# Products of a tile of zeros on TensorE, at the head and around the second normalization of one transformer block

## The chip, the cores and the metric

One core of a Trainium2 chip runs the kernel. A core has five engines, each with a queue of its own that it works off in order: TensorE (PE, matrix products, with its weight loads as PEld), VectorE (DVE), ScalarE (ACT), GpSimd (POOL) and SyncE (SP, which here issues the transfers of the weights). Each waits for the others by semaphores. The metric is the time of one execution on the device in microseconds; lower is better. TensorE's clock has two levels, 1.2 and 2.4 GHz; the profile shows the granted clock as a share of the higher one.

## The reference

One layer of a diffusion transformer in float32: 256 latent tokens and 256 context tokens of 2048 features, 16 heads of 128, and a gated feed-forward part of 5504 features. Cut to what the change touches:

```python
sh1, sc1, g1, sh2, sc2, g2 = adaln(c, w_ada, b_ada)        # silu(c) @ w_ada + b_ada, in six parts
h  = modulate(rms_norm(x, g_mix), sh1, sc1)                # x * (1 + scale) + shift
hc = modulate(rms_norm(ctx, g_mix), csh1, csc1)            # the same of the context
y, _ = neighbourhood_attention(h, hc, w_qkv, ...)          # q, k, v from h; k, v from hc too
x  = x + g1 * y
hf = modulate(rms_norm(x, g_ffn), sh2, sc2)                # the second normalization
x  = x + g2 * conv_ffn(hf, w_up, conv_w, conv_b, w_down)
```

rms_norm divides each token by the root of the mean of its squares over all 2048 features.

## The kernel before, in words

Activations lie with features on the partitions, as 16 blocks of 128 features by 256 tokens. A product of float32 operands is made from high and low parts: `wpair` (L147) loads a weight tile of two blocks of rows by 512 columns over SP, ACT casts it to its high part `wh` (L155), DVE subtracts to get the low part `wl` (L156; two slots). A product is then three: high by high, low by high, high by low. Activations are split the same way: ACT writes the high part (`hh`, L450; `hf`, L817), DVE the low part (L451, L818).

The order in each engine's queue is not the order of the text. A scheduler simulates the program on a time line of its own (L954) and appends each instruction where its simulated time comes, so a change in one place can move instructions of other engines. What the queues hold is fixed when the program is built.

**The head.** `start` code at L485 to L505 streams the latent tokens `xl` in chunks, squares them on ACT (`stats`, L360), adds them on DVE (L365), sums over the partitions on TensorE (`col_sums`, L227) and makes the reciprocal root rstd in `rstd_rows`: scale on DVE (L208), a power on POOL (L195), a Newton step on DVE (L196 to L200), a diagonal matrix (L213, tiles `xd` or `cd`), a product with ones that spreads it over all partitions (L218), a copy (L220, `xb` or `cb`). The context `xc` goes the same way. In parallel `ada_step` (L395) makes shift and scale of one or two blocks: four loads `wx` of `w_ada` (L405, four slots, each of two transfers), four groups of four small products (L411), a copy `ev` on ACT (L418), transposes on TensorE (L421), reductions on DVE (L426 to L434). `modulate` then makes a block of normalized activations (L445 DVE, L450 ACT, L451 DVE), and `first_products` (L459) multiplies it with k and v weights (`nat`: L378, L379, L380). The first block goes alone, the second alone, then pairs. PSUM has eight banks: four under the tag `pj`, two `ms`, two `mx`.

**The second normalization.** Behind the output projection each block gets gate and residual (L778), is squared on ACT (L783) and scaled into `xg` (L788). `col_sums` (L789) takes the last two squares and the sum of the others; `rstd_rows` (L795) makes `yb` the way above, with tile `yd`. A loop over the 16 blocks makes `t` (DVE L815, or POOL L813 for most odd ones), the high part on ACT (L817) and the low part on DVE (L818) of `hf`. The up projection (`proj`, L713, called at L888) follows: each step takes two blocks and eight pairs of products, `wh` with both parts (L728, 512 columns) and `wl` with the high part (L732, 256 columns). The weight splits of L155 and L156 stand in the same queues of ACT and DVE as the loop.

## Time and profile before

| | us |
|---|---|
| Runs | 1459.02, 1455.05, 1456.06 (median 1456.06) |
| Span of the profiled execution, first to last instruction | 1455.1 |
| TensorE busy / weight loads | 1405.5 (97%) / 1166.9 (80%) |
| DVE / ACT / POOL busy | 1004.8 (69%) / 782.6 (54%) / 285.2 (20%) |
| Mean granted clock of TensorE | 0.991 |

Busy time is the time in which an engine works on an instruction; it overlaps between engines. The profile comes from one execution. In the timeline rows the first number is the start, the second the time from the first start to the last end of a group of equal instructions, then engine, line, operation, output and inputs, shapes, and the count; in brackets stands how long the engine was idle ahead of it and what released it. A product is listed with a time longer than its distance to the next, since products are pipelined: the distance of starts is what it costs in a row.

### The profile page before, as it was taken

To read this page: it belongs to the slowest core of one execution; us is meant where nothing else is said; L and a number is where in the kernel's file an instruction comes from. 1 tells how busy PE (TensorE), PEld (TensorE's weight loads), DVE (VectorE), ACT (ScalarE), POOL (GpSimd) and SP (SyncE) were. 2 spreads that over 40 slices of the span, in tenths; PEclk is the share of its full clock that TensorE was granted. 3 is DMA by queue.
4 is the path that set the end of the run, shared out by engine and by line. 5 is a ranking of instruction groups with operands and counts; after the bars stand their busy time and mean duration, and the time that the engine had idled before them with its cause. 6 is when DMAs were issued, how large, how long until landed. Compare 5 with 4: busy or idle time off the path is not lost.

```text
span 1455.1 us, 21097 instructions
## 1 busy us (share of the span) xinstructions
PE 1405.5 (97%) x7608; PEld 1166.9 (80%) x7608; DVE 1004.8 (69%) x1541; ACT 782.6 (54%) x1356; POOL 285.2 (20%) x208
## 2 busy tenths in 40 slices
PE   5999999999998999999899999999999999999998
PEld 2665787778787887788788888888888888888888
DVE  4556587687868778766868878788777775545454
ACT  4322265676565676664656656666665654333333
POOL 1000025465445556200201111111111000000000
PEclk9999999999999999999899999999999999999999
DMA  9999547687667777445567776777776556566554
GB/s 308 357 329 319 176 141 250 199 260 220 213 222 246 223 247 244 151 152 175 183 193 230 224 238 222 244 219 228 233 230 193 183 175 206 185 202 205 167 170 156
DMA packets 208920, 317.14 MB, mean 218 GB/s; under 512 B 23360, under 2 KB 87744, under 8 KB 208816
## 3 DMA queue, kind: packets, MB, share of 16 engines
q1 hardware_dynamic: 208688, 315.79, 68.1%
q8 instruction: 59, 0.97, 0.3%
q14 instruction: 45, 0.37, 0.1%
q10 hardware_dynamic: 128, 0.01, 0.0%
HBM read 312.75 MB, written 3.01 MB: 217 GB/s over the span
## 4 chain that ended last, share of the span: by engine, by line
PE 66%; DVE 12%; issue 10%; DMA 7%; ACT 2%; POOL 2%; SPq 1%; DVEq 0%; POOLq 0%; ACTq 0%
PE pj L728 15%; PE pj L732 8%; PE mx L728 7%; PE ms L728 6%; DVE wl L156 4%; PE pj L379 4%; PE pj L378 4%; PE pj L380 4%; DMA wa<-in_w_ada 4%; PE mx L732 4%; PE ms L732 3%; PE ms L411 2%; PE mx L378 2%; PE mx L379 2%; PE mx L380 2%
## 5 line engine op out<-in xcount | busy, mean ns | idle before, releaser
L156 DVE TENSOR_TENSOR wl<-wr,wh 128x1024 fp32r<-128x1024 f32 (+2 forms) x425 | 496.1, 1168 | 257.0 <-PE pj L732 86.8
L155 ACT CAST wh<-wr 128x1024 fp32r<-128x1024 f32 (+2 forms) x425 | 411.8, 970 | 406.0 <-PE pj L728 150.5
L277 POOL TENSOR_TENSOR acc<-acc,wa 128x512 f32<-128x512 f32 x144 | 226.6, 1573 | 440.9 <-issue 218.1
L728 PE MATMUL pj<-hf,wh 128*128 128x512 f32 x688 | 226.7, 397 | 2.0 <-DVE hf L818 2.0
L379 PE MATMUL pj<-wl,hh 128*128 128x512 f32 x512 | 204.8, 400 | 4.6 <-DVE wl L156 4.5
L380 PE MATMUL pj<-wh,hl 128*128 128x512 f32 x512 | 202.0, 397 | 0.0
L378 PE MATMUL pj<-wh,hh 128*128 128x512 f32 x512 | 194.4, 400 | 2.5 <-ACT hh L450 2.5
L732 PE MATMUL pj<-hf,wl 128*128 128x256 f32 x688 | 154.7, 284 | 2.2 <-DVE wl L156 1.7
L732 PEld LDWEIGHTS pj<-hf,wl 128*128 128x128 f32 x688 | 130.6, 190 | 20.6 <-DVE wl L156 6.2
L728 PEld LDWEIGHTS pj<-hf,wh 128*128 128x128 f32 x688 | 125.3, 190 | 17.7 <-DVE hf L818 2.8
L276 ACT ACTIVATE wa<-wa,sT 128x512 f32<-128x512 f32 x144 | 97.4, 718 | 77.7 <-DMA wa<-in_w_ada 68.1
L728 PE MATMUL mx<-hf,wh 128*128 128x512 f32 x352 | 124.1, 393 | 0.0
L379 PEld LDWEIGHTS pj<-wl,hh 128*128 128x128 f32 x512 | 97.8, 191 | 28.7 <-DVE wl L156 7.9
L728 PE MATMUL ms<-hf,wh 128*128 128x512 f32 x336 | 120.1, 396 | 0.0
L378 PEld LDWEIGHTS pj<-wh,hh 128*128 128x128 f32 x512 | 96.8, 190 | 27.0 <-ACT hh L450 3.4
L380 PEld LDWEIGHTS pj<-wh,hl 128*128 128x128 f32 x512 | 97.6, 191 | 19.5
L732 PE MATMUL mx<-hf,wl 128*128 128x256 f32 x352 | 84.8, 282 | 1.5 <-DVE wl L156 1.5
L279 DVE SCALAR_TENSOR_TENSOR acc<-wa,sT,acc 128x512 f32<-128x512 f32 x80 | 74.4, 931 | 10.7 <-DMA wa<-in_w_ada 10.1
L732 PE MATMUL ms<-hf,wl 128*128 128x256 f32 x336 | 81.7, 282 | 0.0
L732 PEld LDWEIGHTS mx<-hf,wl 128*128 128x128 f32 x352 | 66.3, 188 | 10.4 <-DVE wl L156 3.2
L732 PEld LDWEIGHTS ms<-hf,wl 128*128 128x128 f32 x336 | 63.3, 188 | 7.8
L728 PEld LDWEIGHTS ms<-hf,wh 128*128 128x128 f32 x336 | 63.2, 188 | 6.9
(251 smaller groups left out, 2384.7 us busy)
## 6 DMA issues: line engine op xcount, KB each, us to landing
wr<-in_w_up SPq DMA_DIRECT2D x160, 512.0 KB, 4.4
wa<-in_w_ada SPq DMA_DIRECT2D x128, 512.0 KB, 4.7
wr<-in_w_qkv SPq DMA_DIRECT2D x93, 512.0 KB, 4.9
wr<-in_w_down SPq DMA_DIRECT2D x63, 512.0 KB, 4.6
wx<-in_w_ada SPq DMA_DIRECT2D x56, 512.0 KB, 8.7
wr<-in_w_o SPq DMA_DIRECT2D x24, 512.0 KB, 3.8
wr<-in_w_down SPq DMA_DIRECT2D x45, 256.0 KB, 3.0
wr<-in_w_up SPq DMA_DIRECT2D x16, 384.0 KB, 3.4
```

The lines of the kernel that those rows point to most:

```text
L155: a = nc.scalar.copy(hi[:, :kn, :cn], w[:, :kn, :cn])
L156: b = nc.vector.tensor_tensor(out=lo[:, :kn, :cn], in0=w[:, :kn, :cn], in1=hi[:, :kn, :cn].bitcast(F32), op=ALU.subtract,)
L276: nc.scalar.mul(w[:, k, :], w[:, k, :], s)
L277: nc.gpsimd.tensor_add(acc, acc, w[:, k, :])
L279: nc.vector.scalar_tensor_tensor(out=acc, in0=w[:, k, :], scalar=s, in1=acc, op0=ALU.mult, op1=ALU.add)
L378: nc.tensor.matmul(pt, hh[:, kt, ts], wh[:, k, :], start=a, stop=False)
L379: nc.tensor.matmul(pt, hh[:, kt, ts], wl[:, k, :], start=False, stop=False)
L380: nc.tensor.matmul(pt, hl(kt, ts), wh[:, k, :], start=False, stop=z)
L411: nc.tensor.matmul(ap_[32 * k : 32 * k + 32, :n], s32[:, 4 * q + k, :], w[:, k * n : (k + 1) * n], start=(q == 0), stop=(q == 3), tile_pos ...
L728: nc.tensor.matmul(pts[b][:, : t1 - t0], wh[:, k, bs], mov(kt, slice(t0, t1)), start=(kt == 0 and t0 == 0), stop=False,)
L732: nc.tensor.matmul(pts[b][:, :T], wl[:, k, bs], mov(kt, slice(0, T)), start=False, stop=(kt == kn - 1),)
```

## The change

A tile `warm` of 128x512 zeros is filled on POOL. A helper `spin` issues n products of it (128 columns of it as the stationary operand, all 512 moving) into a PSUM bank whose content nobody reads. With `behind` it is scheduled behind a given instruction; to have these, `col_sums` and `rstd_rows` note their last product in a list `marks`. It is called in six places: 36 products ahead of the first load; 4 behind each of the first three groups of the first adaLN step and 6 behind its transposes; 8 behind the column sums of the second normalization, and 6 behind the product that spreads its rstd. The removed comments move the line numbers (L227 is now L228, L360 L375, L411 L426, L418 L435, L421 L438, L450 L469, L476 L495, L728 L748, L732 L752, L815 L837, L818 L840).

```diff
-    last, hold = [], []
+    last, hold, marks = [], [], []
...
+        ins = nc.tensor.matmul(bp, ones, dg.rearrange("p b t -> p (b t)"), start=True, stop=True)
+        marks.append(ins.ins)
...
+        marks.append(ins.ins)
         return sums
...
+    warm = cp.tile([P, CH], F32R, name="warm")
+    nc.gpsimd.memset(warm.bitcast(F32), 0.0)
+
+    def spin(n, bank, behind=None):
+
+        with ExitStack() as order:
+            if behind is not None:
+                order.enter_context(tc.issue_after(behind))
+            pt = bank()
+            for _ in range(n):
+                ins = nc.tensor.matmul(pt, warm[:, :P], warm, start=True, stop=True)
+        return ins.ins
...
+            if b0 == 0 and q < 3:
+                spin(4, ms, ins.ins)
...
+            ins = nc.tensor.transpose(sp[:, b * P : (b + 1) * P], ev[:, b * P : (b + 1) * P], ident)
+        if b0 == 0:
+            spin(6, ms, ins.ins)
...
+    spin(36, ms)
     stream(xl, xT)
...
     sums2 = col_sums(ms()[:, 0:2], tail)
+    spin(8, pj, marks[-1])
...
     rb2, rb2p, diag = rstd_rows(fp, sums2, "y", nc.scalar.copy)
+    spin(6, pj, marks[-1])
```

Because the scheduler places everything anew, other instructions move too, at the head (up to about 165 us) and behind the second normalization; elsewhere the queues hold the same in the same order.

At the head, this is ACT's queue from the first casts on before. `sq` are squares (of the context chunks `xc`), `hh` the high part of a modulated block, `ev` the adaLN sums out of PSUM, `vsum` a v product out of PSUM.

```order
L155 CAST wh<-wr 128x512 x2
L418 COPY ev<-ms 128x256
L360 ACTIVATE sq<-xc 128x512 x3
L450 ACTIVATE hh<-xl,shT 128x256
L360 ACTIVATE sq<-xc 128x512 x5
L155 CAST wh<-wr 128x512
L476 COPY vsum<-mx 128x512 x2
L418 COPY ev<-ms 128x256
L450 ACTIVATE hh<-xc,shT 128x256
```

And this the same stretch after.

```order
L155 CAST wh<-wr 128x512 x2
L435 COPY ev<-ms 128x256
L375 ACTIVATE sq<-xc 128x512 x8
L469 ACTIVATE hh<-xl,shT 128x256
L155 CAST wh<-wr 128x512
L495 COPY vsum<-mx 128x512 x2
L435 COPY ev<-ms 128x256
L469 ACTIVATE hh<-xl,shT 128x256
```

All eight squares of the context now stand ahead of the first `hh` of the latent tokens, where three stood before.

TensorE's queue from its start to the first product of weights (`wh`, `hh`), after; before, it held the same without the rows of L264.

```order
L264 MATMUL ms<-warm 128x512 x36
L426 MATMUL ms<-wx,s_120 32x256 x4
L228 MATMUL mx<-ones,sacc 128x1 x4
L426 MATMUL ms<-wx,s_120 32x256 x5
L264 MATMUL ms<-warm 128x512 x4
L426 MATMUL ms<-wx,s_120 32x256 x7
L264 MATMUL ms<-warm 128x512 x4
L218 MATMUL mx<-xd,ones 128x256
L264 MATMUL ms<-warm 128x512 x4
L438 MATMUL ms<-ident,ev 128x128 x2
L264 MATMUL ms<-warm 128x512 x6
```

The four products of zeros that belong to the first group stand in the second, and those of the third group behind the spreading product.

TensorE's queue from the end of the first twelve products to the first product of the context's block (`cd` is the diagonal of the context's rstd, `sacc` the squares), before:

```order
L380 MATMUL pj<-wh,hl_110 128x512 x2
L380 MATMUL mx<-wh,hl_110 128x512 x2
L411 MATMUL ms<-wx,s_118 32x256 x4
L227 MATMUL mx<-ones,sacc 128x1 x4
L411 MATMUL ms<-wx,s_118 32x256 x8
L218 MATMUL mx<-cd,ones 128x256
L411 MATMUL ms<-wx,s_118 32x256 x4
L421 MATMUL ms<-ident,ev 128x128 x2
```

And after, to the first product of the next blocks:

```order
L395 MATMUL pj<-wh,hl_112 128x512 x2
L395 MATMUL mx<-wh,hl_112 128x512 x2
L426 MATMUL ms<-wx,s_120 32x256 x12
L228 MATMUL mx<-ones,sacc 128x1 x4
L426 MATMUL ms<-wx,s_120 32x256 x4
L438 MATMUL ms<-ident,ev 128x128 x2
L218 MATMUL mx<-cd,ones 128x256
L426 MATMUL ms<-wx,s_120 32x512 x4
```

The column sums (L227, now L228) moved behind three groups of the next adaLN step, the spreading product (L218) behind the fourth and the transposes, and the first group of the step after that (32x512) ahead of the products.

At the second normalization, TensorE's queue from the last column sums to the first products of the up projection, before:

```order
L227 MATMUL ms<-ones,sacc_5379 128x1 x2
L227 MATMUL ms<-ones,sq 128x1 x4
L218 MATMUL mx<-yd,ones 128x256
L728 MATMUL pj<-hf,wh 128x512
L732 MATMUL pj<-hf,wl 128x256
L728 MATMUL pj<-hf,wh 128x512
```

And after:

```order
L228 MATMUL ms<-ones,sacc_5440 128x1 x2
L228 MATMUL ms<-ones,sq 128x1 x4
L264 MATMUL pj<-warm 128x512 x8
L218 MATMUL mx<-yd,ones 128x256
L264 MATMUL pj<-warm 128x512 x6
L748 MATMUL pj<-hf,wh 128x512
L752 MATMUL pj<-hf,wl 128x256
L748 MATMUL pj<-hf,wh 128x512
```

Eight products of zeros stand between the sums and the spreading product, six behind it.

DVE's queue in the loop over the blocks, from behind the fifth low part on, before:

```order
L818 SCALAR_TENSOR_TENSOR hf<-t,sh2T,hf 128x256
L815 TENSOR_TENSOR t<-xg,yb 128x256
L818 SCALAR_TENSOR_TENSOR hf<-t,sh2T,hf 128x256 x3
L815 TENSOR_TENSOR t<-xg,yb 128x256
L818 SCALAR_TENSOR_TENSOR hf<-t,sh2T,hf 128x256
L156 TENSOR_TENSOR wl<-wr,wh 128x1024
L818 SCALAR_TENSOR_TENSOR hf<-t,sh2T,hf 128x256
L815 TENSOR_TENSOR t<-xg,yb 128x256
L818 SCALAR_TENSOR_TENSOR hf<-t,sh2T,hf 128x256
L815 TENSOR_TENSOR t<-xg,yb 128x256
L818 SCALAR_TENSOR_TENSOR hf<-t,sh2T,hf 128x256
L156 TENSOR_TENSOR wl<-wr,wh 128x1024
```

And after, from the same place:

```order
L840 SCALAR_TENSOR_TENSOR hf<-t,sh2T,hf 128x256
L156 TENSOR_TENSOR wl<-wr,wh 128x1024
L837 TENSOR_TENSOR t<-xg,yb 128x256
L840 SCALAR_TENSOR_TENSOR hf<-t,sh2T,hf 128x256 x3
L837 TENSOR_TENSOR t<-xg,yb 128x256
L156 TENSOR_TENSOR wl<-wr,wh 128x1024
L840 SCALAR_TENSOR_TENSOR hf<-t,sh2T,hf 128x256 x2
L837 TENSOR_TENSOR t<-xg,yb 128x256
L840 SCALAR_TENSOR_TENSOR hf<-t,sh2T,hf 128x256
L156 TENSOR_TENSOR wl<-wr,wh 128x1024
L837 TENSOR_TENSOR t<-xg,yb 128x256
```

The first split of a weight (`wl`) stands behind the tenth `hf` before, and behind the sixth after; the following ones come earlier too.

## Rows read from the trace of the kernel before

**Rows 1.** Busy time, share of the span and number of instructions of TensorE and its weight loads and the other engines, from the page's first part.

```profile
PE 1405.5 (97%) x7608; PEld 1166.9 (80%) x7608; DVE 1004.8 (69%) x1541; ACT 782.6 (54%) x1356; POOL 285.2 (20%) x208
```

**Rows 2.** Windows by stage: stretch and its length, then busy time and instructions of PE, PEld, DVE, ACT and POOL, the granted clock of TensorE as a share of 2.4 GHz, the share of DMA and its GB/s.

```profile
23.00:28.00 5.00, 4.93 (x12) 3.79 (x12) 4.11 (x7) 3.31 (x7) 0.00 (x0) 1.00 1.12 328
28.00:36.00 8.00, 6.30 (x47) 2.46 (x45) 1.98 (x7) 1.85 (x4) 0.70 (x1) 0.79 1.13 322
36.00:53.00 17.00, 17.00 (x88) 10.19 (x87) 8.21 (x22) 7.98 (x14) 0.00 (x0) 1.00 1.08 356
704.00:707.00 3.00, 2.57 (x22) 2.28 (x20) 1.94 (x3) 1.42 (x4) 0.00 (x0) 1.00 0.92 332
707.00:713.00 6.00, 1.60 (x7) 0.83 (x6) 3.79 (x11) 3.48 (x7) 0.73 (x2) 0.54 0.90 305
713.00:717.70 4.70, 4.70 (x15) 4.02 (x16) 4.67 (x9) 2.93 (x7) 2.59 (x3) 0.50 0.50 172
717.70:730.00 12.30, 11.85 (x68) 9.96 (x68) 11.28 (x17) 7.53 (x12) 4.03 (x4) 1.00 0.34 108
```

**Rows 3.** Timeline of PE at the head.

```profile
12.27 1.08 PE L411 MATMUL ms<-wx,s 128*32 128x256 f32 x8 [12.27 <-DMA wx<-in_w_ada]
...
17.66 1.08 PE L411 MATMUL ms<-wx,s 128*32 128x256 f32 x8 [0.65 <-DMA wx<-in_w_ada]
18.66 1.22 PE L218 MATMUL mx<-xd,ones 128*128 128x256 f32 x2
19.95 0.66 PE L421 MATMUL ms<-ident,ev 128*128 128x128 f32 x2
23.07 0.79 PE L378 MATMUL pj<-wh,hh 128*128 128x512 f32 x1 [2.46 <-ACT hh L450]
...
24.09 0.63 PE L378 MATMUL pj<-wh,hh 128*128 128x512 f32 x1
24.51 0.63 PE L379 MATMUL pj<-wl,hh 128*128 128x512 f32 x1
...
28.95 1.05 PE L227 MATMUL mx<-ones,sacc 128*128 128x1 f32 x8
...
31.85 1.08 PE L411 MATMUL ms<-wx,s 128*32 128x256 f32 x8 [1.17 <-DMA wx<-in_w_ada]
32.86 1.22 PE L218 MATMUL mx<-cd,ones 128*128 128x256 f32 x2
...
36.56 0.40 PE L378 MATMUL pj<-wh,hh 128*128 128x512 f32 x1
36.80 0.40 PE L379 MATMUL pj<-wl,hh 128*128 128x512 f32 x1
...
39.95 0.50 PE L378 MATMUL pj<-wh,hh 128*128 128x512 f32 x1
```

**Rows 4.** Waits of PE from 36 to 165 us: what it waited for, us in total, times, the longest.

```profile
PE ms L411 <- DMA wx<-in_w_ada: 0.2, 1, 0.2
```

**Rows 5.** Timeline of PE around the second normalization.

```profile
706.07 1.29 PE L227 MATMUL ms<-ones,sq 128*128 128x1 f32 x8
709.72 1.19 PE L218 MATMUL mx<-yd,ones 128*128 128x256 f32 x2 [2.36 <-issue]
712.95 0.79 PE L728 MATMUL pj<-hf,wh 128*128 128x512 f32 x1 [2.04 <-DVE hf L818]
...
713.75 0.63 PE L728 MATMUL pj<-hf,wh 128*128 128x512 f32 x1
...
714.39 0.63 PE L728 MATMUL pj<-hf,wh 128*128 128x512 f32 x1
...
717.59 0.44 PE L728 MATMUL pj<-hf,wh 128*128 128x512 f32 x1
...
717.99 0.40 PE L728 MATMUL pj<-hf,wh 128*128 128x512 f32 x1
...
718.34 0.40 PE L728 MATMUL pj<-hf,wh 128*128 128x512 f32 x1
...
725.12 0.38 PE L732 MATMUL pj<-hf,wl 128*128 128x256 f32 x1 [0.45 <-DVE wl L156]
```

**Rows 6.** Timeline of POOL at the start: the fill of the mask tile and the last operation of the constants.

```profile
1.05 0.15 POOL L99 MEMSET maskt<- 128x64 f32 x1
...
2.07 0.51 POOL L108 TENSOR_SCALAR_AFFINE_SELECT maskt<-maskt 64x48 f32<-64x48 f32 x2
```

**Rows 7.** Timeline of ACT at the head.

```profile
25.00 1.15 ACT L360 ACTIVATE sq<-xc 128x512 f32<-128x512 f32 x2 [0.35 <-DMA xc<-in_ctxT]
...
35.43 0.51 ACT L450 ACTIVATE hh<-xc,shT 128x256 fp32r<-128x256 f32 x1
```

**Rows 8.** Timeline of DVE at the head, on the way of the context's rstd.

```profile
31.60 0.43 DVE L213 TENSOR_TENSOR cd<-ident,cr 128x256 f32<-128x256 f32 x1
34.12 0.42 DVE L220 COPY cb<-mx 128x256 f32<-128x256 f32 x1 [2.09 <-PE mx L218]
```

**Rows 9.** Timeline of DVE in the loop behind the second normalization: a low part, a `t` and a split of a weight.

```profile
721.39 0.47 DVE L818 SCALAR_TENSOR_TENSOR hf<-t,sh2T,hf 128x256 fp32r<-128x256 f32 x1
721.79 0.41 DVE L815 TENSOR_TENSOR t<-xg,yb 128x256 f32<-128x256 f32 x1
...
723.85 1.22 DVE L156 TENSOR_TENSOR wl<-wr,wh 128x1024 fp32r<-128x1024 f32 x1
```

More of the change, by code (lines that the diff above doesn't have):

```diff
@@ L217, in rstd_rows @@
         bp = mx()[:, :T]
-        nc.tensor.matmul(bp, ones, dg.rearrange("p b t -> p (b t)"), start=True, stop=True)
+        ins = nc.tensor.matmul(bp, ones, dg.rearrange("p b t -> p (b t)"), start=True, stop=True)
+        marks.append(ins.ins)
         rb = pool.tile([P, T], F32, tag=name + "b", name=name + "b")
@@ L226, in col_sums @@
             for b in range(2):
-                nc.tensor.matmul(
+                ins = nc.tensor.matmul(
                     sums[:, b : b + 1], sq[:, b * P : (b + 1) * P], ones[:, 0:1],
@@ L410, in ada_step @@
             for k in range(4):
-                nc.tensor.matmul(
+                ins = nc.tensor.matmul(
                     ap_[32 * k : 32 * k + 32, :n], s32[:, 4 * q + k, :], w[:, k * n : (k + 1) * n],
@@ L420, in ada_step @@
         for b in range(2 * nb):
-            nc.tensor.transpose(sp[:, b * P : (b + 1) * P], ev[:, b * P : (b + 1) * P], ident)
+            ins = nc.tensor.transpose(sp[:, b * P : (b + 1) * P], ev[:, b * P : (b + 1) * P], ident)
+        if b0 == 0:
+            spin(6, ms, ins.ins)
         blk = slice(b0, b0 + nb)
```

## Prediction

> **What bounds the kernel now.** I read the engine shares first: TensorE is busy 97% of the span [rows 1], so nearly every microsecond is products, and a change can win only where TensorE stands still or runs slowly. Next the table by stage with its granted clock [rows 2]: between 36 and 53 us TensorE is busy all of the time at full clock; the two places where it is neither are the head (up to 36 us) and the second normalization (707 to 717.7 us), where the clock column shows 0.54 and 0.50, that is mostly the lower of its two levels, 1.2 instead of 2.4 GHz.
>
> The clock can also be read from the products themselves. At the head, starts are 0.43 us apart at 24 us (24.09, 24.51) and 0.24 at 36.56 and 36.80 [rows 3], although the clock column says 1.00 between 23 and 28 us [rows 2]. By the column the head has nothing to win before 28 us; by the pitch its first twelve products, 5.3 us from 23.07 on, ran at 1.2 GHz and could win 2.5. I go by the pitch. The Trainium skill, page "TensorE: Matmul & The Clock Gate", section "Part 1: The HAM clock gate (the "warmup" mystery)", says that the throttled level is the default and that activity releases it; by that rule the head could come out 2.5 us faster, by the column 0. The pitch agrees with the rule, the column does not.
>
> Then who waits for whom. Head: TensorE starts at 12.27 when the first adaLN weights land, waits for the fourth tile until 17.66, and for the first modulated block until 23.07 [rows 3]. After 36 us it waits 0.2 us in all of the next 129 us [rows 4]: a delay that the head leaves is handed on one to one. Second normalization: the column sums end at 707.36, the product that spreads rstd over the partitions starts at 709.72, the up projection at 712.95; its pairs of products come every 0.64 us (713.75, 714.39) at first and every 0.35 us (717.99, 718.34) later [rows 5].
>
> **The change at the head.** *36 products of zeros first.* Their tile is filled on POOL, behind the last mask operation, which ends at 2.6 us; a 128x64 fill took 0.15 us [rows 6], eight times that is 1.2 at most, so they begin between 2.6 and 3.8. A product of this shape costs 0.43 or 0.24 us, 36 of them 8.6 to 15.5. At the second normalization the clock rose behind 4.64 us of products (712.95 to 717.59 [rows 5]); with as many slow ones here, 11 go at 0.43 and 25 at 0.24: 10.7 us, end at 13.3 to 14.5, one or two us behind 12.27. That is hidden: the fourth adaLN group waits for its weights until 17.66 whatever the others do. Cost 0.
>
> *The products between.* Four and four come in the gaps ahead of the spreading product (18.66), four ahead of the transposes (19.95), six behind them: 14 x 0.24 = 3.4 us, of which at most 0.6 delays the transposes and none the first product, because that waits for other engines until 23.07. Cost 0 by themselves.
>
> *What the scheduler made of it costs more.* In the new order ACT squares all eight chunks of the context before it makes the first modulated block; before, three came first. The chunks arrive as they arrive: the last two are squared from 25.00 on, 1.15 us for both, and a modulated block took 0.51 [rows 7]. So the first product moves from 23.07 to 25.00 + 1.15 + 0.51 = 26.7, **3.6 us late**, and TensorE, done with its zeros by about 22.6, has stood idle for four microseconds; I take the clock to be low again (at the second normalization it went down as TensorE stopped [rows 2, 5]). The twelve products end at 29.5 at full clock or 31.9 at low. That delay alone would be partly absorbed: before, TensorE then waited 1.17 us for weights at 31.85. But behind it the order of the context's normalization is also worse. Its column sums, at 28.95 before [rows 3], now stand behind three adaLN groups, the third of which needs the tile that landed at 31.85 (perhaps a little earlier, since the queue now asks for one more of these tiles ahead of the first split weight): start 32.4 to 33.6. And its spreading product, at 32.86 before, ahead of the fourth group, now stands behind that group and its transposes, which wait for a copy on ACT. From the sums' start, the chain to the first product took 36.0 - 28.95 = 7.0 us (sums to 30.00, the scaled diagonal to 32.03, spread to 34.12, copy, modulate and ACT to 35.94 [rows 3, 7, 8]), with about 1 us of wait in it. 6 to 7 us from 32.4 to 33.6 gives 38.4 to 40.6 for the first product of the context. From there the products take 2.8 us. Before, that work was done at 39.95, one adaLN group included that the new order has already run in the wait. Lag: 38.4 + 2.8 - 39.95 = 1.3 to 40.6 + 2.8 - 39.95 = 3.5, and up to 1 us more if these products run at 1.2 GHz for some time. Value **+3.0 us**, range +1.3 to +4.2; above the middle, since each of the three late things (squares, sums, spread) stands in one row. Nothing gives it back: TensorE is fully busy until 165 us.
>
> **The change at the second normalization.** *Eight products of zeros behind the sums.* TensorE stands idle for 2.36 us here, 707.36 to 709.72 [rows 5]. Eight at full clock are 1.9 us: hidden, done before the product that spreads rstd. At low clock they take 3.4 us and delay it by 1.1. The column's 0.54 over 707 to 713 [rows 2] is about 0.5 us at full clock and 5.5 at half: it fell near 707.5, after the sums had ended, and was full before [rows 2]; the zeros leave no idle time behind the sums, so I take the full clock.
>
> *Six behind the spreading product*: 1.4 us (2.6 at low clock) in a gap of 2.04 us (710.91 to 712.95 [rows 5]). Hidden at full clock.
>
> *What it buys.* If TensorE stays at full clock, the seven cold pairs (712.95 to 717.59, 4.64 us) take 7 x 0.35 = 2.45: 2.2 us saved. The spreading product took 1.19 us at low clock; at half that, 0.6 comes off ahead of everything. Together up to 2.8, and 0.3 more if the wait of 0.45 us at 725.12 for a low part goes too: bound -3.1.
>
> *What is late next.* DVE, which makes the low parts of activations and weights, is busy 4.67 of 4.70 us while the products are slow, and 11.28 of 12.30 after [rows 2]. A TensorE 2.8 us ahead would meet it: the low part that TensorE awaited at 725.12 was made from 723.85 on [rows 9]. In the old order the gain would stop there. But the order of DVE has changed with the simulated faster products: the first of these splits stands behind the 6th high-low pair instead of the 10th, some 3 us earlier, and its slots come free with the products. Laid out with durations from rows (0.47 a low part, 0.41 a t, 1.22 a split [rows 9], steps of eight pairs at 2.8 us), DVE keeps up with a new wait of 0.2 to 0.5 us. Value **-2.3 us**, range -3.1 to -1.0 (only half of the pairs come out fast), at worst +1.6 (below).
>
> Elsewhere, from 165 us on, each engine's order is the same. The sum is +3.0 - 2.3 = **+0.7 us**: span 1455.1 + 0.7 = 1455.8. The median of the runs shown (1456.06) lies 0.96 above the profiled span, so 1456.8 for the median. A difference under 0.3% (4.4 us) can't be told from none in a measurement of this kernel.
>
> **The rivals.**
>
> 1. *The head costs nothing and the second normalization gives all.* For it: DMA engines are fully busy until 53 us and beyond [rows 2], so arrivals may set the pace and the lag may be absorbed by earlier weights. Against: after 36 us TensorE waits 0.2 us for a weight [rows 4], so there is no wait to shorten. Time 1456.1 - 3.1 = 1453.0 to 1453.8 with the middle value: 16%. A head that is faster by the 2.5 us of its slow first products as well: 1450.6, 4%.
>
> 2. *Slower: the eight zeros run at 1.2 GHz.* The mechanism sits at 707.4 us: eight at 0.43 take 3.4 us in a gap of 2.36, the spreading product starts 1.1 late, six more at 0.43 take 2.6 in a gap of 2.04, and the first product of the up projection starts 1.6 late and no warmer. It decides from a pitch of 2.36 / 8 = 0.29 us on. For it: the clock was low from 707.5 on, 0.1 us after the sums, so it may have been on its way down with them. With the head at +3.0: 1456.06 + 4.6 = 1460.7. 12%.
>
> 3. *Zeros don't raise the clock at all.* Then 36 x 0.43 = 15.5 us push the first adaLN group from 12.27 to about 18.5, the head comes out about 12 us late, the second normalization 1.6: 1470. No row shows a product of zeros. 3%.
>
> **How the numbers follow.** Forecast 65%: 1456.8. The rivals have 16, 4, 12 and 3. Its own range: head +1.3 to +4.2, second normalization -3.1 to -1.0, mostly 1454.5 to 1459. Reaching to rival 1's middle and rival 2's edge leaves out about 15%: 1453.0 to 1460.5. Faster by over 0.3% (under 1451.7): 5%. Slower by over 0.3% (over 1460.4): 10%, rival 3 and the larger half of rival 2. The same: 85%.
>
> **What would show it.** Head right: 36 products end near 13 to 14 us; the first product of weights at about 26.7, behind ACT; the context's sums later than 32; TensorE's queue at the work of 39.95 about 3 us later. Head wrong: first product at 23 or earlier, or the lag gone by 100 us. Second normalization right: eight starts 0.24 apart, the up projection's first pairs 0.35 apart, granted clock near 1.00 from 707 to 718, DVE's first split some 3 us earlier. Wrong: pairs still 0.64 apart, or waits of over 1 us for low parts before 730 us. The prediction falls as a whole if TensorE is idle after 36 us for more than the lag, or if the head's first product isn't late.

## The result

The changed kernel took **1459.82 us** (median of 20 runs), the kernel before 1455.48 us (20 runs, measured beside it): ratio **1.003, 95% interval 1.002 to 1.0039**. It is slower, by about 4.3 us. The profiled execution has a span of 1459.1 us; before, 1455.1 us.

First the engine shares, to hold against [rows 1]:

```profile
PE 1418.4 (97%) x7676; PEld 1176.5 (81%) x7676; DVE 1002.2 (69%) x1541; ACT 782.6 (54%) x1356; POOL 281.2 (19%) x209
```

68 more products (36 + 12 + 6 + 8 + 6 of zeros), 13 us more of busy TensorE, and the share is still 97%. What counts is where they lie. Windows by stage (columns as in [rows 2], the second normalization shifted by the lag):

```profile
23.00:28.00 5.00, 1.75 (x8) 1.10 (x7) 4.75 (x10) 3.54 (x7) 0.00 (x0) 1.00 1.12 330
...
36.00:53.00 17.00, 15.66 (x70) 8.20 (x70) 6.00 (x17) 6.22 (x12) 0.00 (x0) 0.81 1.09 353
...
718.00:735.00 17.00, 16.58 (x90) 13.73 (x88) 16.36 (x27) 11.75 (x22) 7.38 (x7) 0.99 0.55 176
```

Between 23 and 28 us TensorE is now busy 1.75 us instead of 4.93, and between 36 and 53 us no longer all of the time and no longer at full clock (0.81 instead of 1.00). At the second normalization the loop runs at 0.99 from 718 us on. So the head lost and the second normalization gained; the timelines say how much. TensorE at the head, against [rows 3]:

```profile
2.64 11.08 PE L264 MATMUL ms<-warm 128*128 128x512 f32 x36 [2.64 <-POOL warm L255]
13.65 0.64 PE L426 MATMUL ms<-wx,s 128*32 128x256 f32 x8
...
26.74 0.50 PE L393 MATMUL pj<-wh,hh 128*128 128x512 f32 x1 [3.25 <-ACT hh L469]
27.08 0.40 PE L394 MATMUL pj<-wl,hh 128*128 128x512 f32 x1
27.32 0.39 PE L393 MATMUL pj<-wh,hh 128*128 128x512 f32 x1
...
32.62 0.64 PE L426 MATMUL ms<-wx,s 128*32 128x256 f32 x8 [1.17 <-DMA wx<-in_w_ada]
33.19 1.05 PE L228 MATMUL mx<-ones,sacc 128*128 128x1 f32 x8
...
38.77 1.94 PE L426 MATMUL ms<-wx,s 128*32 128x512 f32 x8 [0.54 <-DMA wx<-in_w_ada]
40.64 0.79 PE L393 MATMUL pj<-wh,hh 128*128 128x512 f32 x1
41.23 0.63 PE L394 MATMUL pj<-wl,hh 128*128 128x512 f32 x1
41.66 0.63 PE L393 MATMUL pj<-wh,hh 128*128 128x512 f32 x1
...
44.36 1.06 PE L426 MATMUL ms<-wx,s 128*32 128x512 f32 x8
```

Read it downwards. The 36 products of zeros are done at 13.65 and the adaLN groups go on behind them. The first product of weights waits 3.25 us for ACT and starts at 26.74 instead of 23.07. Its clock is high: the next two starts, 27.08 and 27.32, are 0.24 apart, where before they were 0.43. In spite of that the context's column sums start at 33.19 instead of 28.95 and its first product at 40.64 instead of 36; that product and the next go at 0.43 again (41.23, 41.66). The work that was done at 39.95 before is done at 44.36: **4.4 us late**. At 168 us the lag between the two profiled executions is 6.2 us; of the 1.8 us between, one new wait for a low part accounts for 0.4, the rest is not assigned. How far such a number can be trusted: e1, e6, e7 and e8 below have no zeros at the head and the queue of before there on TensorE, and their profiled executions lag by -0.05, 0.96, 1.66 and 0.07 us at 168 us.

What held the first product up, in the timelines of ACT ([rows 7] before) and DVE:

```profile
25.14 1.15 ACT L375 ACTIVATE sq<-xc 128x512 f32<-128x512 f32 x2 [0.30 <-DVE sacc L380]
26.20 0.49 ACT L469 ACTIVATE hh<-xl,shT 128x256 fp32r<-128x256 f32 x1
...
25.05 0.48 DVE L464 SCALAR_TENSOR_TENSOR xl<-xl,gsT,xb 128x256 f32<-128x256 f32 x1
```

The modulated block stands directly behind the last square. DVE was nearly as late: its part of the block, at 21.32 before, now stands behind four adds of the context's squares and ends at 25.5. So the late squares on ACT are not the only thing that moved ahead of this block; without them it would have come some 0.7 us earlier here.

Now the second normalization on TensorE, against [rows 5]:

```profile
712.79 1.29 PE L228 MATMUL ms<-ones,sq 128*128 128x1 f32 x8
713.94 3.05 PE L264 MATMUL pj<-warm 128*128 128x512 f32 x8
716.79 1.05 PE L218 MATMUL mx<-yd,ones 128*128 128x256 f32 x2
717.28 2.17 PE L264 MATMUL pj<-warm 128*128 128x512 f32 x6
719.88 0.50 PE L748 MATMUL pj<-hf,wh 128*128 128x512 f32 x1 [0.42 <-DVE hf L840]
...
720.33 0.40 PE L748 MATMUL pj<-hf,wh 128*128 128x512 f32 x1
...
720.69 0.40 PE L748 MATMUL pj<-hf,wh 128*128 128x512 f32 x1
...
735.34 0.38 PE L752 MATMUL pj<-hf,wl 128*128 128x256 f32 x1 [0.20 <-DVE wl L156]
```

From the sums to the spreading product are 4.00 us (3.65 before), to the first pair 7.09 (6.88 before), then the pairs come every 0.36 us at once (720.33, 720.69), where seven of them took 4.64 us before. The lag of 6.7 us at the sums is 4.6 at 731 us: **2.1 us gained**. Ahead of the sums TensorE waited 1.28 us for DVE (0.33 before; 1.51 in e2, which has no zeros here), so the lag had just risen from 5.8; counted from there the gain is 1.2. At the end of the program the lag is 4.0 us (1459.1 - 1455.1), near the 4.3 of the medians.

### The profile page after: what moved, and what is told of

Its sections match the earlier page's. It is cut to its first block, busy times and chain, and to the rows that moved or that the text cites. A ratio compares the mean times of both kernels' runs of the same rounds, so it can differ in the third digit from the quotient of the medians.

```text
span 1459.1 us, 21228 instructions
## 1 busy us (share of the span) xinstructions
PE 1418.4 (97%) x7676; PEld 1176.5 (81%) x7676; DVE 1002.2 (69%) x1541; ACT 782.6 (54%) x1356; POOL 281.2 (19%) x209
## 4 chain that ended last, share of the span: by engine, by line
PE 65%; DVE 13%; DMA 10%; issue 3%; ACT 3%; POOL 3%; SPq 1%; DVEq 0%; POOLq 0%; ACTq 0%
PE pj L748 16%; PE pj L752 9%; PE mx L748 8%; PE ms L748 7%; DMA wa<-in_w_ada 6%; DVE wl L156 5%; PE mx L752 4%; PE ms L752 4%; PE pj L394 3%; PE pj L393 2%; PE pj L395 2%; POOL acc L292 2%; PE ms L426 2%; PE mx L393 2%; PE mx L394 2%
## 5 line engine op out<-in xcount | busy, mean ns | idle before, releaser
L292 POOL TENSOR_TENSOR acc<-acc,wa 128x512 f32<-128x512 f32 x144 | 221.7, 1540 | 436.2 <-issue 218.8
L748 PE MATMUL pj<-hf,wh 128*128 128x512 f32 x688 | 224.8, 395 | 0.4 <-DVE hf L840 0.4
L752 PE MATMUL pj<-hf,wl 128*128 128x256 f32 x688 | 153.8, 283 | 2.0 <-DVE wl L156 1.4
L752 PEld LDWEIGHTS pj<-hf,wl 128*128 128x128 f32 x688 | 129.5, 188 | 20.2 <-DVE wl L156 5.9
L748 PEld LDWEIGHTS pj<-hf,wh 128*128 128x128 f32 x688 | 124.3, 188 | 15.6 <-DVE hf L840 0.9
L748 PE MATMUL mx<-hf,wh 128*128 128x512 f32 x352 | 124.2, 393 | 0.0
L748 PE MATMUL ms<-hf,wh 128*128 128x512 f32 x336 | 120.1, 396 | 0.0
L752 PE MATMUL mx<-hf,wl 128*128 128x256 f32 x352 | 84.8, 282 | 1.5 <-DVE wl L156 1.5
L752 PE MATMUL ms<-hf,wl 128*128 128x256 f32 x336 | 81.8, 282 | 0.0
L752 PEld LDWEIGHTS mx<-hf,wl 128*128 128x128 f32 x352 | 66.3, 188 | 10.4 <-DVE wl L156 3.2
L752 PEld LDWEIGHTS ms<-hf,wl 128*128 128x128 f32 x336 | 63.3, 188 | 7.9
L748 PEld LDWEIGHTS ms<-hf,wh 128*128 128x128 f32 x336 | 63.2, 188 | 6.9
```

The costliest lines, as they stand in the source:

```text
L292: nc.gpsimd.tensor_add(acc, acc, w[:, k, :])
L748: nc.tensor.matmul(pts[b][:, : t1 - t0], wh[:, k, bs], mov(kt, slice(t0, t1)), start=(kt == 0 and t0 == 0), stop=False,)
L752: nc.tensor.matmul(pts[b][:, :T], wl[:, k, bs], mov(kt, slice(0, T)), start=False, stop=(kt == kn - 1),)
```

## The experiments

The theory at the start: the loss is in the head, and it comes from the order that the scheduler chose when it counted the zeros (squares first, the context's sums and spreading product behind adaLN groups), not from the products of zeros. The rivals: the zeros themselves delay something, or the second normalization brought nothing. Diffs are against the changed kernel; line numbers differ a little from kernel to kernel. "Lag" is by how much a profiled execution is behind the profiled execution of the kernel before at the same work.

### e1: only the second normalization

```diff
-            if b0 == 0 and q < 3:
-                spin(4, ms, ins.ins)
-        if b0 == 0:
-            spin(6, ms, ins.ins)
-    spin(36, ms)
```

> Only the eight and six products of zeros at the second normalization; the head is that of before. In the changed kernel the lag fell from 6.7 us at the column sums to 4.6 us at 731 us, 2.1 us. If that gain belongs to the zeros (theory): lag 0 up to 705 us, about -2 us at 730 and at the end, 1453.5 against 1455.5, the first pairs of the up projection 0.35 apart. If it was only made possible by a head that came late, so that DVE and the transfers were further ahead (rival): within 0.5 us of before, with new waits for low parts of 1.5 us or more between 718 and 730 us.

Measured: ratio 0.9977 [0.9962, 0.9993], 1452.63 us. In its profile no lag at 168 us (-0.04), and between the sums and 731 us a gain of 1.9 us. TensorE there:

```profile
708.84 3.44 PE L264 MATMUL pj<-warm 128*128 128x512 f32 x8
...
712.57 1.76 PE L264 MATMUL pj<-warm 128*128 128x512 f32 x6
```

The eight take 3.44 us, 0.43 each: they run at the low clock. The six take 0.29 each, and the pairs come at full clock (0.35 apart). The second part of the change alone is a gain.

### e2: only the head

```diff
-    spin(8, pj, marks[-1])
-    spin(6, pj, marks[-1])
```

> Only the zeros of the head. Theory and rival both expect the whole loss of the head here: first product of weights at 26.7 us, a lag of about 6 us at 165 us. The end tells how the two places add: 1455.5 + 4.5 + 2 = 1462 if what the second normalization gives back is its own, about 1460 if the lag shrinks there by itself.

Measured: ratio 1.0033 [1.002, 1.0046], 1459.7 us; lag 5.6 us at 168 us, and from the sums of the second normalization to 731 us nearly unchanged (5.65 to 5.09), with pairs 0.64 us apart as before. The loss is the head's. In this execution the first twelve products ran at the low clock (from 27.78 on, 0.43 apart, after 3.58 us without work), and the context's first product started at 40.65 all the same, as in the changed kernel (40.64).

### e3: the new order without any zeros

```diff
+    with tc.issue_after(squares[-1]):
+        modulate(*GRAINS[0], ((0, xl),))
...
+            if b0 == 1 and q == 2:
+                with tc.issue_after(ins.ins):
+                    rb.append(sum_up(csq, "c")[0])
...
+            with tc.issue_after(marks[-2]) if b0 == 1 and q == 3 else ExitStack():
...
-    spin(36, ms)
-    spin(8, pj, marks[-1])
-    spin(6, pj, marks[-1])
```

(and the products between are left out.)

> No product of zeros anywhere, but the order of the changed kernel at the head, forced by hand: all eight squares of the context ahead of the first modulated block, the context's column sums behind three adaLN groups of the next step, its spreading product behind the fourth and the transposes. Theory (the order makes the loss): first product of weights at 26 to 27 us, lag of 5 to 8 us at 165 us (more than in the changed kernel by what low clock costs), 1460 to 1464. Rival (the zeros themselves make it, by standing in TensorE's queue and putting the first adaLN group 1.4 us later): first product late, but the lag gone by 165 us, 1455 to 1457.

Measured: ratio 1.0018 [1.0008, 1.0028], 1459.59 us, lag 4.2 us at 168 us. The head is late without one product of zeros: first product at 27.02, sums at 33.64, first product of the context at 39.93. The lag is less than was expected of the order (5 to 8 us).

### e4: all zeros, the squares and the last group put back

```diff
-            nc.scalar.activation(sq, xin[:, kt : kt + 2, :], AF.Square)
+            with tc.issue_after(gate[0]) if gate and kt >= 6 else ExitStack():
+                nc.scalar.activation(sq, xin[:, kt : kt + 2, :], AF.Square)
...
+            with tc.issue_after(marks[-1]) if b0 == 1 and q == 3 else ExitStack():
```

> All products of zeros as in the changed kernel, but the order of before at the head as far as it matters: three squares of the context, then the first modulated block, then the rest; the context's column sums behind one adaLN group, its spreading product behind three. Theory: first product of weights at 23 to 24 us at full clock, no lag or up to 2.5 us of lead at 165 us, and the 2 us of the second normalization on top: 1451 to 1453.5. Rival: the lag of 5 to 6 us at 165 us stays, 1459 to 1460.

Measured: ratio 0.9999 [0.9991, 1.0008]. Better than the change, short of e1; the time lies between what the theory and the rival expected. TensorE:

```profile
16.67 1.82 PE L264 MATMUL ms<-warm 128*128 128x512 f32 x4
...
21.35 0.59 PE L218 MATMUL mx<-xd,ones 128*128 128x256 f32 x2
...
25.47 0.50 PE L394 MATMUL pj<-wh,hh 128*128 128x512 f32 x1 [0.89 <-ACT hh L471]
...
41.53 1.06 PE L428 MATMUL ms<-wx,s 128*32 128x512 f32 x8 [1.69 <-DMA wx<-in_w_ada]
```

Here the zeros between take time in the queue: four of them at the low clock take 1.8 us, and the spreading product starts at 21.35 (18.66 before). The first product starts at 25.47 (23.07), but not by that alone: on DVE two adds of the context's squares, 0.68 us each, stand ahead of its part of the block (24.39; 21.32 before). The adaLN group behind the context's products is on time all the same (38.78; 38.96 before): the warm products have made up the 2.4 us. Then a wait of 1.69 us for weights, ahead of 41.53, makes the kernel late again.

### e5: few zeros, in the old order

```diff
-            if b0 == 0 and q < 3:
-                spin(4, ms, ins.ins)
         if b0 == 0:
-            spin(6, ms, ins.ins)
+            spin(4, ms, ins.ins)
-    spin(36, ms)
+    spin(24, ms)
```

> Zeros at the head that leave the order of before in every queue as it was, but for one spreading product and one diagonal that move by one place: 24 first and four behind the transposes, together with the eight and six at the second normalization. Theory (order made the head's loss; the zeros cost nothing, and the arrival of weights at 28 and 32 us eats what warm products win): first product of weights near 23 us at full clock, TensorE then waits for a tile of adaLN weights near 28 and 32 us, lag at 165 us between -0.7 and +0.3, end as with the zeros of the second normalization alone, 1453 to 1454. Rival (zeros cost something by themselves): lag of +1.5 to +3 at 165 us, 1455 to 1457. Second rival (the warm products' 2.5 us are kept): lag -2.5 at 165 us, 1451.

Measured: ratio 0.9979 [0.9965, 0.9993], the same as e1. TensorE:

```profile
13.62 1.08 PE L426 MATMUL ms<-wx,s 128*32 128x256 f32 x8 [3.56 <-DMA wx<-in_w_ada]
...
24.80 0.50 PE L393 MATMUL pj<-wh,hh 128*128 128x512 f32 x1 [2.21 <-ACT hh L467]
25.13 0.39 PE L394 MATMUL pj<-wl,hh 128*128 128x512 f32 x1
...
30.01 1.03 PE L426 MATMUL ms<-wx,s 128*32 128x256 f32 x8 [2.19 <-DMA wx<-in_w_ada]
```

The first adaLN tile happened to land at 13.62 instead of 12.27, so all is a good microsecond late. The first products run at full clock (24.80 to 25.13 and on at 0.23), and what that wins is waited away: 2.19 us for weights ahead of 30.01. Not all of this wait speaks of warm products, since that group is 1.6 us late (28.38 before) with the late first tile. The lag at 168 us is 2.1 us, as the rival that zeros cost something had it; the time is the theory's.

### e6: the earlier split of a weight undone

e1 with the first split in the loop behind the tenth low part, as before:

```diff
+        if kt == 9:
+            late_low.append(low.ins)
...
+                if len(seen) > 1:
+                    order.enter_context(tc.issue_after(late_low[0]))
```

> Zeros at the second normalization alone, with DVE's first split of a weight put back behind the tenth low part, where it stood before. Theory of the prediction (without the earlier split DVE would stop the gain): waits for low parts of weights of 1 to 2 us together between 718 and 731 us, the gain from the column sums to 731 us shrinks from 1.9 us to 0.5 or less, 1454.5 to 1456. Rival (DVE has room either way): the same waits as with the zeros alone, gain 1.5 to 2, 1453 to 1454.

Measured: ratio 0.9994 [0.998, 1.0008]; the gain is gone, and the profile is 1.0 us later over the stage (lag 2.05 to 3.08).

```profile
723.85 0.42 PE L751 MATMUL pj<-hf,wl 128*128 128x256 f32 x1 [1.99 <-DVE wl L160]
724.08 0.62 PE L747 MATMUL pj<-hf,wh 128*128 128x512 f32 x1
724.49 0.63 PE L751 MATMUL pj<-hf,wl 128*128 128x256 f32 x2
```

TensorE, now faster, catches up with DVE, waits 1.99 us for a low part, and after that wait the clock is low again (0.41 between the last two starts).

### e7 and e8: one group of zeros at a time

e1 with only the eight, and with only the six:

```diff
-    spin(6, pj, marks[-1])
```

> Only the eight zeros behind the column sums; every queue has otherwise the order of before. With both groups the eight ran mostly at the lower clock (3.44 us), and the clock was up again near 712.7 us, as the second group began. If the second group or its place matters: idle TensorE ahead of the up projection again, its first pairs 0.64 us apart, the spreading product 0.5 to 1 us late, end 0 to +1 us against before. If eight are enough: pairs at 0.35, end about -1.5 us.

Measured: ratio 0.9997 [0.9981, 1.0013], lag over the stage 4.83 to 5.17. The pairs start warm and fall:

```profile
718.18 0.50 PE L743 MATMUL pj<-hf,wh 128*128 128x512 f32 x1 [2.04 <-DVE hf L834]
...
719.51 0.63 PE L743 MATMUL pj<-hf,wh 128*128 128x512 f32 x1
...
720.15 0.63 PE L743 MATMUL pj<-hf,wh 128*128 128x512 f32 x1
```

The 2.04 us without work ahead of 718.18 is what the six cover.

```diff
-    spin(8, pj, marks[-1])
```

> Only the six zeros behind the spreading product. They begin at the lower clock and take 2.6 us in a gap of 2.04, so the first pair is up to 0.6 us late; if the clock rises as long after the start of dense work as before, some four of the seven slow pairs become fast: +0.6 - 1.2 = -0.6 us, 1455. If only both groups together do it: seven slow pairs still, +0.5 us.

Measured: ratio 0.9987 [0.9974, 1.0]; lag over the stage 0.79 to 0.03. Between no change and e1, and not told apart from either. TensorE:

```profile
711.14 2.82 PE L264 MATMUL pj<-warm 128*128 128x512 f32 x6
...
725.15 0.39 PE L747 MATMUL pj<-hf,wl 128*128 128x256 f32 x1 [0.95 <-DVE wl L156]
```

The six ran 0.44 us each, held the first pair up by less than 0.1 us (713.80), and the pairs came at 0.35: the lag fell from 0.79 to -1.36 us at the work of 717.99. Then two waits for low parts of weights took it back, 0.63 us ahead of 721.12 and 0.95 ahead of 725.15. The first split in the loop stands 6.06 us behind the first pair here and 3.98 in the changed kernel. So the six alone bring the clock up as well; what they lack in this run is the earlier split, as in e6.

### e9: only the late squares

No zeros; the first modulated block behind all eight squares, the context's sums, spreading product and last group in the old places:

```diff
+    with tc.issue_after(squares[-1]):
+        modulate(*GRAINS[0], ((0, xl),))
...
+            with tc.issue_after(marks[-1 if q == 3 else -2]) if b0 == 1 and q in (1, 3) else ExitStack():
```

> No product of zeros; of the changed kernel's order at the head only the first piece: all eight squares of the context ahead of the first modulated block. The context's column sums and spreading product stand where they stood before (one and three adaLN groups ahead of them). Theory (a late first product alone is absorbed, since TensorE then waits for adaLN weights at 28 and 32 us; the moved sums and spreading product make the loss): first product at 26.5 to 27 us, the context's first product at 36 to 38 us, lag at 165 us +0.5 to +2.5, 1456 to 1457.5. Rival (the late squares make it): lag +4 at 165 us as in the kernel with the whole order, 1459.

Measured: ratio 1.0026 [1.0013, 1.0038], lag 6.06 us at 168 us.

```profile
26.96 0.79 PE L398 MATMUL pj<-wh,hh 128*128 128x512 f32 x1 [5.98 <-ACT hh L471]
...
33.29 1.05 PE L228 MATMUL mx<-ones,sacc 128*128 128x1 f32 x8
...
36.51 1.17 PE L218 MATMUL mx<-cd,ones 128*128 128x256 f32 x2 [1.17 <-DVE cd L213]
...
41.67 0.80 PE L398 MATMUL pj<-wh,hh 128*128 128x512 f32 x1
```

The theory expected 0.5 to 2.5 us of lag and failed; its rival came. The squares alone give as large a loss as the whole order (e3) or all zeros of the head (e2). The sums have their old place in the queue, behind the twelve products and one group, and start at 33.29 all the same, because what is ahead of them is late. The wait of 1.17 us for weights at 31.85 before is gone; a wait of 1.17 us for the context's diagonal, ahead of 36.51, stands in its place. One more thing moved: the first group of the step after stands ahead of the context's products (39.80), as in the changed kernel. e11 has that too (38.52) and is not slower.

### e10: the wait of e4 taken away

e4 with the second group of the third step held behind products of the context:

```diff
+                prods.append(nc.tensor.matmul(pt, hl(kt, ts), wh[:, k, :], start=False, stop=z).ins)
...
+            with tc.issue_after(marks[-1] if b0 == 1 else prods[-4]) if (b0, q) in ((1, 3), (2, 1)) else ExitStack():
```

> The kernel with all zeros and the order of before at the head, in which TensorE still waited 1.69 us at 41.5 us for an adaLN group (the second of the third step) that its scheduler had put ahead of the products; here that group is put back behind some products, about where it stood before. Theory (the lag of 2.95 us at 165 us came from this place, as there was none at 38.8 us): no such wait, lag at 165 us 0 to +1.2, end 1453 to 1454 as with the zeros of the second normalization alone. Rival (the zeros themselves): lag stays near +3, 1455.5.

Measured: ratio 1.001 [0.9994, 1.0025]. The wait at 41.5 is gone from the profile, the time is not better, and the lag at 168 us is 3.5 us: as the rival expected, that the zeros themselves cost it. But in this execution the context's products ran at the low clock (from 36.31 on, 0.43 apart), which they did not in e4, so the run does not decide it. That this wait was e4's loss is not borne out.

### e11: only the moved sums

No zeros, the squares in the old order; the context's sums behind three groups, its spreading product behind the fourth and the transposes:

```diff
+            if b0 == 1 and q == 2:
+                with tc.issue_after(ins.ins):
+                    rb.append(sum_up(csq, "c")[0])
...
-    spin(36, ms)
```

> No product of zeros; of the changed kernel's order at the head only the second piece: the context's column sums behind three adaLN groups of the next step and its spreading product behind the fourth and the transposes. Three squares of the context stand ahead of the first modulated block, as before. The squares alone gave +4 us or more. If the moved sums cost something by themselves (the prediction's reading): first product at 23 us, the context's first product at 38.5 to 40 us instead of 36, lag at 165 us +2.5 to +4, 1457.5 to 1459. If the late squares are the whole cause (new theory): lag within 1.5 us of before, 1455 to 1456.5.

Measured: ratio 0.9998 [0.9985, 1.0011], no change. Yet at 45 us its profile is nearly as late as that of the changed kernel:

```profile
23.60 0.79 PE L399 MATMUL pj<-wh,hh 128*128 128x512 f32 x1 [2.45 <-ACT hh L475]
...
32.95 1.05 PE L228 MATMUL mx<-ones,sacc 128*128 128x1 f32 x8
...
40.39 0.80 PE L399 MATMUL pj<-wh,hh 128*128 128x512 f32 x1
```

3.44 us of lag at 168 us, -0.88 at 704 us, and nothing in the median. The expected time came, the expected lag (within 1.5 us) did not. A lag read at the head of one profiled execution is therefore no safe measure of the median.

### e12: e4 without the products between

36 first, eight and six at the second normalization, gates as in e4:

```diff
-            if b0 == 0 and q < 3:
-                spin(4, ms, ins.ins)
-        if b0 == 0:
-            spin(6, ms, ins.ins)
```

> 36 zeros first and those of the second normalization, none between the adaLN groups or behind the transposes, and the order of before at the head but for small moves. In the kernels with the zeros between and the order of before the first product came at 25.4 us instead of 23.1, since the four and four run at 1.2 GHz (2.1 us for four) ahead of the spreading product, which came at 21.3 instead of 18.7. If these zeros are what keeps those kernels 3 us behind the one with zeros at the second normalization alone: spreading product by 19.5, first product at 23 to 24 us, lag at 165 us within 1 us of before, 1452.5 to 1454. If not: 1455 to 1456.5.

Measured: ratio 0.9978 [0.9961, 0.9995], as e1 and e5. First product at 23.95, at the low clock again (24.54 and 24.96, 0.42 apart).

```profile
23.95 0.79 PE L394 MATMUL pj<-wh,hh 128*128 128x512 f32 x1 [1.67 <-ACT hh L467]
24.54 0.63 PE L395 MATMUL pj<-wl,hh 128*128 128x512 f32 x1
24.96 0.63 PE L394 MATMUL pj<-wh,hh 128*128 128x512 f32 x1
```

e12 and e4 differ by the products between and by what the scheduler moved with them: 0.9978 against 0.9999, some 3 us, the intervals just overlap. In e12 the spreading product starts at 21.21, hardly earlier than in e4, behind the transposes; the difference ahead of the first product is on DVE, where the block's part (22.84) stands ahead of the adds of the context's squares. How much of the 3 us is the time of the products between is not shown. The lag of 3.6 us at 168 us is more than was expected (1 us).

## Why the prediction came out as it did

The time lies in the stated range, 3 us above the forecast, and at the edge of what was called no change; the interval of the ratio tells it from none. It lies above the forecast's own range (1454.5 to 1459): the stated one held it because it reached up to rival 2, and the price of that rival (a spreading product 1.1 us late, pairs no warmer) was not paid in this run. So the range was met in part by luck. The forecast change was +0.7 us, the measured one is +4.3. The signs were right in both places; a step of the head's sum failed, and its size was too small.

**Right: what bounds the first product.** Forecast 26.7 behind the last square, measured 26.74; that DVE's part of the block was late too (25.5) the forecast did not see. The 36 were forecast to end between 13.3 and 14.5; they ended at 13.65. They hid, as costed: e5 and e12, with zeros first, are as fast as e1 without.

**Wrong: the clock of the first twelve products.** "I take the clock to be low again" at 26.7; they ran 0.24 us apart (in e2, with the same zeros at the head, they were slow, as forecast). That should have helped. It didn't, because the groups ahead of the sums then wait for weights: in the timeline, 1.17 us ahead of 32.62. e2 confirms it: with slow first products the context's first product starts at 40.65, here at 40.64. So the 2.5 us that the head's slow products seemed to offer could not be had: with warm products the next tile of weights is late instead.

**The step that failed: "That delay alone would be partly absorbed".** e9 has that delay, and its lag is 6.06 us and its ratio 1.0026. The wait for weights that was to absorb it did go, but the wait of 1.17 us for the context's diagonal took its place: TensorE works its queue in order, and the context's sums stand behind the twelve late products (33.29 instead of 28.95); so do the context's rstd, its modulated block and its products. (A shorter delay was absorbed: in e4 the first product is 2.4 us late, its products are warm, and at 38.78 there is no lag.) The prediction put the rest of the head's loss on the moved sums and spreading product; e11 moves these alone and is not slower (0.9998). The order makes a loss without one zero (e3: 1.0018), and its costly part is the block behind the squares.

**The term mis-sized: the head, +3.0 with a bound of +4.2.** By the profile it is 4.4 at 44.36; e2, the head alone, has +0.33% [0.20, 0.46] in the ratio, 4.8 us. The bound does not follow from its own terms: 3.5 and up to 1 us more are 4.5. The context's first product starts at 40.64, the upper end of 38.4 to 40.6: of the chain from the sums (7.45 us instead of 6 to 7) the group at 38.77 is a part, 1.94 us at the low clock behind a wait of 0.54, not "in the wait". And the first products behind it ran at the low clock until 42.08, so the twelve took 3.72 us instead of 2.8: the "up to 1 us more" of the bound.

**Cost 0 for the products between: not borne out, and not refuted.** They are 18, where the sum took 14 x 0.24. In the changed kernel the first product waits for ACT until 26.74, and for DVE until 25.5, whatever stands ahead on TensorE. With the squares put back (e4) the spreading product is 2.7 us later than before and the first product 2.4; but part of that is DVE's order, and e12, without these products, has its spreading product as late. Against e12 e4 loses some 3 us, not certain by the intervals. The rival that "the zeros themselves cost" stays open by that.

**Right: the second normalization, -2.3 forecast, -2.1 in the profile, -1.9 in e1's; e1's ratio is -0.23% [-0.38, -0.07], 3.3 us.** The reason was partly wrong. The eight did not keep the full clock: 3.05 us here, 3.44 in e1, as the rival of slow zeros had it, and the clock column says 0.60 from 714 to 718 us where 1.00 was forecast. But the spreading product was only 0.35 us later and the first pair 0.21, and the clock was back before the pairs. So that rival's premise held and its price did not. It differs from execution to execution: in e5 the eight took 2.09 us, as forecast, and the gain from the sums to 731 us is 2.8; in e10 they made the spreading product 1.5 us later, and 1.0 is left. What the pairs need is work right ahead of them: with the eight alone, TensorE stands still for 2.04 us and the clock falls within the first pairs (e7); with the six alone the pairs are warm (e8). The Trainium skill, page "TensorE: Matmul & The Clock Gate", section "Part 1: The HAM clock gate (the "warmup" mystery)", says that the throttled level is the default and that activity releases it. e1 and e8 agree, with products of zeros as the activity: pairs 0.35 us apart behind them, 0.64 before.

**Right: what is late next.** The first split in the loop stands 3.98 us behind the first pair instead of 7.31, and the one new wait is 0.20 us (735.34). With the old place of the split the gain stops at DVE (e6: 1.99 us of wait, and a low clock behind it).

**"Nothing gives it back" is not shown beyond 165 us.** e11's and e12's lags of 3.4 and 3.6 us at 168 us are gone by 704 us. Part of that is the single execution of before: 1.6 us of it is a stretch at the low clock between 260 and 264 us that e11 and e12 don't have (last section).

**What stays open.** Head alone and second normalization alone add to 0.33 - 0.23 = +0.10%; measured together they are +0.30% [0.20, 0.39]. The order without zeros (e3) and the second normalization add to less still, 0.18 - 0.23 = -0.05%, and that gap is wider than the intervals. So either the zeros at the head cost something in the changed kernel too, or the second normalization gains less behind a late head. The profile has the gain in both, the median hardly. Three terms of about 0.2% each (order +, products between +, second normalization -) fit every run with its interval, the change with +0.2% at the lower end of its own; that is a fit, not a proof, and it charges the products between in the changed kernel, where the first product waited for other engines. The profiles give a hint and no more: between 44 and 168 us the lag grows by 1.8 us in the changed kernel and by 2.0 in e2, and by 0.3 in e3, which has no zeros. Which work pays for the rest of the 4.3 us is open.

## What to carry to other kernels

Products that only keep TensorE's clock up are worth something where TensorE really stands still and the engine that feeds the next work keeps pace: here eight and six of them around one normalization, 0.23% (e1). Where the next thing is bound by arriving weights, they bring nothing. And when a scheduler simulates the program to choose its order, compare each other engine's order after such an edit: here ACT's squares moved ahead of the block that TensorE waited for, which alone costs about as much (0.26%, e9) as the products gain; a version that holds the order (e5) or leaves the head alone (e1, 1452.63 us) beats both kernels.

## What the runs showed of the hardware beyond this

The same short pauses of TensorE in the attention part lower the clock in one execution and not in another. Two stretches in windows of the kernel before (columns as in [rows 2]):

```profile
255.00:270.00 15.00, 12.92 (x57) 10.32 (x56) 9.88 (x16) 10.71 (x17) 6.76 (x5) 0.89 0.74 221
535.00:565.00 30.00, 26.90 (x132) 21.75 (x131) 26.45 (x45) 20.15 (x55) 21.78 (x16) 1.00 0.64 208
```

The same stretches in windows of the changed kernel, whose work is some 5 us further back in them:

```profile
255.00:270.00 15.00, 12.22 (x58) 9.97 (x58) 7.14 (x13) 11.14 (x18) 7.10 (x6) 1.00 0.65 199
535.00:565.00 30.00, 25.39 (x113) 20.27 (x112) 22.34 (x40) 21.47 (x64) 18.26 (x13) 0.89 0.67 212
```

TensorE stands still for 2.1 us in the first stretch before and for 2.8 after, and the clock falls before (0.89) and not after; in the second it is 3.1 and 4.6 us, and the clock falls after. Between 260 and 264 us, where only the kernel before runs at the low clock, the lag of the changed kernel falls from 6.2 to 4.6 us; over the second stretch, with its longer pause, it rises from 1.9 to 6.5. So single profiles differ by some microseconds without a cause in the edit. e11's lag of 3.4 us goes at the first of these pauses, where e11 doesn't pause and keeps the full clock.

Early in an execution the clock column can't be trusted. In e11, without zeros, it says 1.00 from 23 to 28 us while products of 128x512 start 0.43 us apart; in e12, where 36 of zeros ran first, it says 0.50 there for products 0.42 apart. The pitch tells the clock in both.

TensorE could start on the first tile of weights at 12.27 us before and at 13.62 in e5, with the same transfers queued ahead.
